# A rotary embedding in fp32: one signed GpSimd product per tile, and PSUM copies of two banks

## The chip, the cores and the metric

One core of a Trainium2 chip runs the kernel. The metric is the device time of one execution in microseconds (us), the median of several runs. The profile's span, from the first to the last instruction of one execution, is about 2 us shorter than that time. Runs come fast or slow; only fast runs are compared.

## The reference

```python
# x: 8 x 2048 x 8 x 64, cos and sin: 2048 x 32, all fp32
x1 = x[..., :32]
x2 = x[..., 32:]
out1 = x1 * cos - x2 * sin
out2 = x1 * sin + x2 * cos
return np.concatenate([out1, out2], axis=-1)
```

Input and output are 33.5 MB each, the tables 0.5 MB together. Every element costs two products and one sum.

## The kernel before

Each of the eight batches is one buffer of 128 x 8192 elements (4.2 MB). SyncE's queue loads five buffers ahead, ScalarE's queue stores each batch from the same buffer, and the load of batch b+5 waits for the store of batch b. A batch is worked off in tiles, most of 2048 elements per partition. PSUM is the memory into which TensorE writes its sums; a bank is here a stretch of it of 512 elements per partition. Of each tile VectorE computes t1 = x * cos and GpSimd t2, the other half of x times sine, with a minus sign for the first half of each head. Then the two are added, in one of three ways:

- kind A: VectorE adds t1 (in PSUM) and t2.
- kind B: TensorE adds them by two matmuls with the identity, and ScalarE copies the sum from PSUM.
- kind C: VectorE computes t2 too; TensorE adds, ScalarE copies. GpSimd has no part.

The first tile of batches 1 and 3 is of kind C, that of batches 2, 4 and 5 of kind B, all others of kind A.

```python
    o_pool = ctx.enter_context(tc.tile_pool(name="op", bufs=2, space=PSUM))
    ...
    keep(nc.scalar.mul(nsin, sin_sb, -1.0))
    keep(nc.scalar.copy(sin_ps, sin_sb))
    ...
        if kind != "C":
            for u, tab in ((1, sin_sb), (0, nsin)):
                keep(
                    nc.gpsimd.tensor_mul(
                        out=t2u[:, :, u, :].rearrange("p (r h) d -> p r h d", h=H),
                        in0=xu[:, :, 1 - u, :].rearrange("p (r h) d -> p r h d", h=H),
                        in1=rep(tab[:, r0 : r0 + nr, :], H),
                    )
                )
        keep(nc.vector.tensor_mul(out=..., in0=xk, in1=rep(cos_ps[...], 2 * H)))   # t1
        if kind == "A":
            keep(nc.vector.tensor_add(out=xt, in0=t1, in1=t2))
        elif kind == "B":
            for j in range(n // C):                       # C = 512 elements, one bank
                o = o_pool.tile([P, C], f32, tag="o")
                cs = slice(j * C, (j + 1) * C)
                nc.tensor.matmul(o, eye, t1[:, cs], start=True, stop=False)
                nc.tensor.matmul(o, eye, t2[:, cs], start=False, stop=True)
                keep(nc.scalar.copy(xt[:, cs], o))
        ...
```

## Time and profile before

| | before |
|---|---|
| time, median of the 3 runs known at first | 164.34 us (164.15 to 164.58) |
| span of the profiled run | 162.0 us |
| busy: VectorE, GpSimd, TensorE, ScalarE | 140.1, 138.9, 46.6, 14.3 us |
| bytes moved | 67.65 MB, mean 418 GB/s |
| 16 DMA engines, both data queues | 98.0% of the span |

Three things are close together here: VectorE, GpSimd and the DMA are all busy for over 85% of the span. A share of the whole span doesn't say which of them sets the end. That takes the view by windows, which shows whether a resource is full in every stretch, and the view of waits, which shows who stands still for whom. The prediction below quotes both.

### The profile page before, as it was taken

How to read it: one execution, taken by the hardware profiler on the slowest of the kernel's cores; microseconds unless marked ns; L12 is line 12 of the kernel's file. 1: busy time of each engine (PE TensorE's matmuls, PEld its weight loads, DVE VectorE, ACT ScalarE, POOL GpSimd, SP SyncE). 2: the span in 40 equal slices, each digit the busy share in tenths (PEclk: the TensorE clock that was granted, in tenths of full speed). 3: DMA queues.
4: the chain of work that ended last, by engine and by line, in shares of the span. 5: the costliest groups of instructions: out<-in, count | busy, mean ns of one | idle time of the engine just before them, and what ended most of it. 6: DMA issues, size and time to landing. Idle time of an engine off the chain costs nothing.

```text
span 162.0 us, 463 instructions
## 1 busy us (share of the span) xinstructions
PE 46.6 (29%) x80; PEld 18.6 (11%) x80; DVE 140.1 (86%) x66; ACT 14.3 (9%) x24; POOL 138.9 (86%) x70
## 2 busy tenths in 40 slices
PE   0000000499008920894039913980000000000000
PEld 0000000143004400340023401330000000000000
DVE  0468999999999999999999999499989999899930
ACT  3200000013100410022001210130000000000000
POOL 1299999999999899983999979999799979999600
PEclk9999999999965997599855895799555555555555
DMA  5999999989899999999999999999999999999994
GB/s 176 419 441 494 413 388 502 372 380 429 388 477 429 396 485 413 405 494 396 421 477 396 429 463 396 453 453 388 453 447 405 445 445 405 453 437 405 417 421 198
DMA packets 3170, 67.65 MB, mean 418 GB/s; under 512 B 352, under 2 KB 352, under 8 KB 608
## 3 DMA queue, kind: packets, MB, share of 16 engines
q1 hardware_dynamic: 1728, 34.08, 49.9%
q10 hardware_dynamic: 1440, 33.56, 48.1%
q14 instruction: 2, 0.02, 0.0%
HBM read 34.08 MB, written 33.55 MB: 417 GB/s over the span
## 4 chain that ended last, share of the span: by engine, by line
DMA 47%; DVE 37%; POOL 9%; issue 2%; SPq 1%; DVEq 0%; POOLq 0%; ACTq 0%
DMA xt<-in_x_dram 26%; DVE t L128 18%; DMA out_dram<-xt 18%; DVE xt L135 17%; POOL t L121 9%; DMA sin_sb<-in_sin_dram 3%; DVE t L145 1%; SPq L69 0%; SPq L67 0%; DVEq L135 0%; POOLq L121 0%; ACTq L74 0%
## 5 line engine op out<-in xcount | busy, mean ns | idle before, releaser
L121 POOL TENSOR_TENSOR t<-xt,sin_sb 128x1024 f32<-128x1024 f32 (+1 forms) x32 | 70.5, 2203 | 12.8 <-DMA xt<-in_x_dram 6.4
L128 DVE TENSOR_TENSOR t<-xt,cos_ps 128x2048 f32<-128x2048 f32 (+1 forms) x34 | 73.4, 2167 | 0.8
L121 POOL TENSOR_TENSOR t<-xt,nsin 128x1024 f32<-128x1024 f32 (+1 forms) x32 | 70.6, 2207 | 0.0
L135 DVE TENSOR_TENSOR xt<-t,t 128x2048 f32<-128x2048 f32 (+1 forms) x29 | 62.2, 2145 | 8.1 <-POOL t L121 5.6
L140 PE MATMUL o<-t,eye 128*128 128x512 f32 x24 | 16.3, 766 | 24.0 <-DVE t L128 24.0
L156 PE MATMUL o<-t,eye 128*128 128x512 f32 x16 | 11.3, 812 | 38.1 <-DVE t L128 38.1
L141 PE MATMUL o<-t,eye 128*128 128x512 f32 x24 | 15.3, 725 | 0.0
L142 ACT COPY xt<-o 128x512 f32<-128x512 f32 x12 | 7.0, 585 | 44.8 <-PE o L141 44.8
L140 PEld LDWEIGHTS o<-t,eye 128*128 128x128 f32 x24 | 5.6, 249 | 32.5 <-issue 32.5
L156 PEld LDWEIGHTS o<-t,eye 128*128 128x128 f32 x16 | 3.8, 257 | 43.0 <-POOL t L121 30.6
L161 ACT COPY xt<-o 128x512 f32<-128x512 f32 x8 | 4.7, 586 | 44.7 <-DVE t L128 26.6
L141 PEld LDWEIGHTS o<-t,eye 128*128 128x128 f32 x24 | 5.7, 239 | 8.0 <-issue 8.0
L92 DVE COPY cos_ps<-cos_sb 128x512 f32<-128x512 f32 x1 | 0.7, 694 | 6.3 <-DMA cos_sb<-in_cos_dram 6.3
L157 PE MATMUL o<-t,neye 128*128 128x512 f32 x8 | 5.3, 766 | 0.2 <-DVE t L145 0.2
L145 DVE TENSOR_TENSOR t<-xt,sin_ps 128x2048 f32<-128x2048 f32 x2 | 4.6, 2281 | 0.0
L157 PE MATMUL o<-t,eye 128*128 128x512 f32 x8 | 4.1, 592 | 0.0
L157 PEld LDWEIGHTS o<-t,neye 128*128 128x128 f32 x8 | 1.9, 258 | 4.1 <-issue 4.1
L157 PEld LDWEIGHTS o<-t,eye 128*128 128x128 f32 x8 | 1.5, 190 | 1.9 <-issue 1.9
L89 ACT ACT_TABLE_LOAD x1 | 1.3, 1283 | 0.7 <-PEq L197 0.7
L89 ACT ACTIVATE nsin<-sin_sb 128x512 f32<-128x512 f32 x1 | 0.6, 629 | 4.9 <-DMA sin_sb<-in_sin_dram 4.9
L90 ACT COPY sin_ps<-sin_sb 128x512 f32<-128x512 f32 x1 | 0.6, 579 | 0.0
L79 POOL MEMSET eye<- 128x128 f32 x1 | 0.2, 204 | 0.3 <-POOLq L197 0.3
(6 smaller groups left out, 1.0 us busy)
## 6 DMA issues: line engine op xcount, KB each, us to landing
xt<-in_x_dram SPq DMA_DIRECT2D x7, 4096.0 KB, 42.0
out_dram<-xt ACTq DMA_DIRECT2D x7, 4096.0 KB, 25.7
xt<-in_x_dram SPq DMA_DIRECT2D x2, 1024.0 KB, 6.1
xt<-in_x_dram SPq DMA_DIRECT2D x1, 2048.0 KB, 11.5
out_dram<-xt ACTq DMA_DIRECT2D x1, 2048.0 KB, 10.8
out_dram<-xt ACTq DMA_DIRECT2D x2, 1024.0 KB, 7.1
cos_sb<-in_cos_dram SPq DMA_DIRECT2D x1, 256.0 KB, 5.1
sin_sb<-in_sin_dram SPq DMA_DIRECT2D x1, 256.0 KB, 5.3
```

Of the source, the lines that this page charges most:

```text
L89: keep(nc.scalar.mul(nsin, sin_sb, -1.0))
L92: keep(nc.vector.tensor_copy(cos_ps, cos_sb))
L121: nc.gpsimd.tensor_mul(out=t2u[:, :, u, :].rearrange("p (r h) d -> p r h d", h=H), in0=xu[:, :, 1 - u, :].rearrange("p (r h) d -> p r h d" ...
L128: nc.vector.tensor_mul(out=t1.rearrange("p (r k d) -> p r k d", r=nr, d=Dh), in0=xk, in1=rep(cos_ps[:, r0 : r0 + nr, :], 2 * H),)
L135: keep(nc.vector.tensor_add(out=xt, in0=t1, in1=t2))
L140: nc.tensor.matmul(o, eye, t1[:, cs], start=True, stop=False)
L141: nc.tensor.matmul(o, eye, t2[:, cs], start=False, stop=True)
L142: keep(nc.scalar.copy(xt[:, cs], o))
L145: nc.vector.tensor_mul(out=t2.rearrange("p (r k d) -> p r k d", r=nr, d=Dh), in0=xk, in1=rep(sin_ps[:, r0 : r0 + nr, :], 2 * H),)
L156: nc.tensor.matmul(o, eye, t1u[:, gs, u, :], start=True, stop=False)
L157: nc.tensor.matmul(o, eye if u else neye, t2u[:, gs, 1 - u, :], start=False, stop=True)
L161: nc.scalar.copy(xu[:, gs, u, :], o.rearrange("p (g d) -> p g d", d=Dh))
```

## The change

The intent is to have GpSimd issue one instruction per tile in place of two, by means of a table that holds minus sine and plus sine in turns and a read of the input that takes the second half of each head first (a step of -32). Besides, ScalarE copies two PSUM banks in one instruction in place of one. For the room this takes, the two PSUM buffers of one bank become one buffer of two banks.

```diff
-    o_pool = ctx.enter_context(tc.tile_pool(name="op", bufs=2, space=PSUM))
+    o_pool = ctx.enter_context(tc.tile_pool(name="op", bufs=1, space=PSUM))
 ... (cos_sb and sin_sb move into a pool that is free at the start)
-    nsin = const_pool.tile([P, R, Dh], f32, tag="ns")
+    sgn = const_pool.tile([P, R, 2, Dh], f32, tag="sg")
 ...
-    keep(nc.scalar.mul(nsin, sin_sb, -1.0))
+    for lo, hi in ((0, 4), (4, R)):
+        keep(nc.scalar.mul(sgn[:, lo:hi, 0, :], sin_sb[:, lo:hi, :], -1.0))
+        keep(nc.scalar.copy(sgn[:, lo:hi, 1, :], sin_sb[:, lo:hi, :]))
 ...
+    def swapped(a, nr):
+        return dataclasses.replace(
+            a,
+            offset=a.offset + Dh,
+            ap=[a.ap[0][:], [HD, nr], [D, H], [-Dh, 2], [1, Dh]],
+        )
+
+    def signed(a, nr):
+        return dataclasses.replace(
+            a, ap=[a.ap[0][:], [D, nr], [0, H], [Dh, 2], [1, Dh]]
+        )
 ...
-            for u, tab in ((1, sin_sb), (0, nsin)):
-                keep(
-                    nc.gpsimd.tensor_mul(
-                        out=t2u[:, :, u, :].rearrange("p (r h) d -> p r h d", h=H),
-                        in0=xu[:, :, 1 - u, :].rearrange("p (r h) d -> p r h d", h=H),
-                        in1=rep(tab[:, r0 : r0 + nr, :], H),
-                    )
+            keep(
+                nc.gpsimd.tensor_mul(
+                    out=t2.rearrange("p (r h u d) -> p r h u d", r=nr, h=H, u=2),
+                    in0=swapped(xt, nr),
+                    in1=signed(sgn[:, r0 : r0 + nr, :, :], nr),
                 )
+            )
 ... (kind B; kind C alike)
-            for j in range(n // C):
-                o = o_pool.tile([P, C], f32, tag="o")
-                cs = slice(j * C, (j + 1) * C)
-                nc.tensor.matmul(o, eye, t1[:, cs], start=True, stop=False)
-                nc.tensor.matmul(o, eye, t2[:, cs], start=False, stop=True)
-                keep(nc.scalar.copy(xt[:, cs], o))
+            for j in range(n // (2 * C)):
+                o = o_pool.tile([P, 2 * C], f32, tag="o")
+                for k in range(2):
+                    cs = slice((2 * j + k) * C, (2 * j + k + 1) * C)
+                    oc = o[:, k * C : (k + 1) * C]
+                    nc.tensor.matmul(oc, eye, t1[:, cs], start=True, stop=False)
+                    nc.tensor.matmul(oc, eye, t2[:, cs], start=False, stop=True)
+                keep(nc.scalar.copy(xt[:, 2 * j * C : 2 * (j + 1) * C], o))
```

More of the change, by code (lines that the diff above doesn't have):

```diff
@@ L46 @@
     t2_pool = ctx.enter_context(tc.tile_pool(name="t2p", bufs=3))
-    cos_sb = const_pool.tile([P, R, Dh], f32, tag="cb")
-    sin_sb = const_pool.tile([P, R, Dh], f32, tag="sb")
-    nsin = const_pool.tile([P, R, Dh], f32, tag="ns")
+    cos_sb = t1s_pool.tile([P, R, Dh], f32, tag="t1s", name="cos_sb")
+    sin_sb = t1s_pool.tile([P, R, Dh], f32, tag="t1s", name="sin_sb")
+    sgn = const_pool.tile([P, R, 2, Dh], f32, tag="sg")
     eye = const_pool.tile([P, P], f32, tag="eye")
@@ L152, in rotate @@
             for u in range(2):
+                o = o_pool.tile([P, n // 2], f32, tag="o")
                 for j in range(n // 2 // C):
-                    o = o_pool.tile([P, C], f32, tag="o")
+                    oc = o[:, j * C : (j + 1) * C]
                     gs = slice(j * G, (j + 1) * G)
-                    nc.tensor.matmul(o, eye, t1u[:, gs, u, :], start=True, stop=False)
+                    nc.tensor.matmul(oc, eye, t1u[:, gs, u, :], start=True, stop=False)
                     nc.tensor.matmul(
-                        o, eye if u else neye, t2u[:, gs, 1 - u, :], start=False, stop=True
+                        oc, eye if u else neye, t2u[:, gs, 1 - u, :], start=False, stop=True
                     )
-                    keep(
-                        nc.scalar.copy(
-                            xu[:, gs, u, :], o.rearrange("p (g d) -> p g d", d=Dh)
-                        )
+                keep(
+                    nc.scalar.copy(
+                        xu[:, :, u, :], o.rearrange("p (g d) -> p g d", d=Dh)
                     )
+                )
     def pieces(b):
```

## The prediction

> **What bounds the kernel now.** GpSimd is the second-busiest engine of the page (138.9 us of a 162.0 us span), and the change works on it, so the first question is whether GpSimd sets the end at all. I read the page's slices and DMA queues first.
>
> ```profile
> POOL 1299999999999899983999979999799979999600
> DMA  5999999989899999999999999999999999999994
> DMA packets 3170, 67.65 MB, mean 418 GB/s; under 512 B 352, under 2 KB 352, under 8 KB 608
> q1 hardware_dynamic: 1728, 34.08, 49.9%
> q10 hardware_dynamic: 1440, 33.56, 48.1%
> ```
>
> To see: the 16 DMA engines are at nine tenths or more in all but four of 40 slices. The two data queues together take 98.0% of the engines' time, 0.98 x 162.0 = 158.8 us. GpSimd has holes (8 and 3 together, then 7, 7, 7), about one every 19 us from the middle on. Is the DMA really full, or full on the average only? The view by windows answers (columns: window, its length, busy time of PE, PEld, DVE, ACT and POOL, granted clock, DMA share, GB/s):
>
> ```profile
> 0.00:5.00 5.00, 0.00 (x0) 0.00 (x0) 0.00 (x0) 1.28 (x1) 0.70 (x6) 1.00 0.64 216
> 5.00:155.00 150.00, 46.65 (x80) 18.60 (x80) 139.83 (x66) 13.06 (x23) 138.24 (x64) 0.76 1.00 430
> 155.00:160.00 5.00, 0.00 (x0) 0.00 (x0) 0.28 (x1) 0.00 (x0) 0.00 (x0) 0.50 0.96 406
> 160.00:162.00 2.00, 0.00 (x0) 0.00 (x0) 0.00 (x0) 0.00 (x0) 0.00 (x0) 0.50 0.03 12
> ```
>
> To see: share 1.00 at 430 GB/s for 150 us on end, and 0.96 until 160. What is not full is the first load's start (5 us at 0.64, so some 1.8 us lost) and the last store's completion (2 us). The 67.65 MB are the input once, the output once and the tables; at 430 GB/s that is 157.3 us, plus these ends of some 4 us: the span. Then the chain that ended last (start, length, what):
>
> ```profile
> 7.03 9.48 POOL t L121 x6
> 16.51 0.02 issue
> 16.53 2.30 DVE xt L135
> ...
> 63.05 28.39 DMA out_dram<-xt
> ...
> 91.57 42.01 DMA xt<-in_x_dram
> ...
> 133.71 4.62 POOL t L121 x2
> ...
> 154.05 1.23 DVE xt L135
> ```
>
> To see: GpSimd stands in it at two places only, 9.5 us at the start and 4.6 us after the last load; in between it is VectorE and then 70 us of one store and one load. The chain names compute after 133.7 us, but the windows show the DMA full there too: it works off stores that wait. The view of GpSimd's waits:
>
> ```profile
> POOL t L121 <- DMA xt<-in_x_dram: 6.4, 4, 3.4
> POOL t L121 <- DMA sin_sb<-in_sin_dram: 5.7, 1, 5.7
> POOL t L121 <- DVE xt L135: 0.5, 1, 0.5
> ```
>
> To see: GpSimd has caught up with the loads in the second half and waits for input, four times, at 75.6, 95.0, 114.4 and 133.7 us by the timeline, 19.36 us apart. Making it faster there only makes it wait longer. **The DMA engines are the bound.**
>
> **What the Trainium skill says.** (1) "DMA: Bandwidth & Descriptors", Specifications, gives a fabric ceiling of 435 GB/s and about 358 GB/s of HBM per core. The trace's 430 GB/s agrees with the first and passes the second, so I take the DMA to be at its ceiling. (2) "GPSIMD Engine Reference", Elementwise — side-by-side cycle accounting, has a two-input fp32 operation over 2048 elements at 4497 ns on GpSimd and 2293 ns on VectorE. The trace has 2292 ns on VectorE; GpSimd runs two instructions of 1024 per tile so far. (3) The same page, Performance pitfalls for Q7 kernels, has reads half again as dear where the inner step is over 8 bytes. The new read's negative step is in the second dimension (-32 elements); the inner step remains one fp32, 4 bytes, so this should not bite. No row of the trace before has a negative step, so it is not tested. (4) "SBUF — State Buffer", Who interferes with whom: a VectorE instruction with two SBUF inputs holds up GpSimd's reads. Here one VectorE input is always in PSUM, and its 2292 ns shows no hindrance; the change leaves that as it is.
>
> **The change part by part.**
>
> *GpSimd.* The groups by form:
>
> ```profile
> L121 POOL TENSOR_TENSOR t<-xt,nsin 128x1024 f32<-128x1024 f32 x28 | 65.6, 2341 | 0.0
> L121 POOL TENSOR_TENSOR t<-xt,sin_sb 128x1024 f32<-128x1024 f32 x28 | 65.4, 2337 | 7.0 <-DMA xt<-in_x_dram 6.4 <-DVE xt L135 0.5
> L121 POOL TENSOR_TENSOR t<-xt,nsin 128x512 f32<-128x512 f32 x4 | 5.1, 1266 | 0.0
> L121 POOL TENSOR_TENSOR t<-xt,sin_sb 128x512 f32<-128x512 f32 x4 | 5.1, 1264 | 5.7 <-DMA sin_sb<-in_sin_dram 5.7
> ```
>
> Records overlap a little, so I count from start to start in the timeline: 2.28 us for 1024 elements, 1.21 us for 512. So 1.07 us per 512 elements and 0.14 us fixed. One instruction of 2048 then starts the next after 0.14 + 4 x 1.07 = 4.42 us, in place of 2 x 2.28 = 4.56: 0.14 us less per tile, since only the fixed part goes; the elements are as many as before. The 64 products become 32 (28 of 2048, 4 of 1024), so 32 x 0.14 = 4.5 us less busy: 138.9 to about 134.4 us. Nearly all of it turns into waits for loads.
>
> *The start.* The first product now needs the signed table. Before, it started when the sine table had landed (7.03 us). Now ScalarE first writes two pieces of 128 elements; the 128-element multiply took 0.30 us, and a second behind it perhaps 0.25. So it starts near 7.5 us, 0.45 late. Then 2.28 + 2.28 + 4.42 = 8.98 us until the third tile's product, at 16.5 us: just where it was (16.51). From there VectorE sets the pace (4.73 us per tile), so the first store is issued at 28.3 us as now. The rest of the table, the PSUM copy of sine and the negated identity are needed only after that.
>
> *TensorE and ScalarE.* A 512-element PSUM copy takes 0.585 us; the 512- and 128-element multiplies (0.629 and 0.299 us) give 0.86 ns per element, so 1024 take about 1.03 us. 20 x 0.585 = 11.7 us become 10 x 1.03 = 10.3. But there is now one PSUM buffer of two banks in place of two of one, so the second pair of chunks waits for the first copy: about 1.1 us of TensorE idle, and a last copy some 1.6 to 2 us later in each of the five tiles. The tightest is batch 4: its last copy ended at 94.6 us; now about 96.2; its store was issued at 97.74, after VectorE's last add. It still fits. The order of instructions and their waits on GpSimd and TensorE are otherwise those of before, tile for tile; the same one waits for TensorE to release a product buffer.
>
> *The end.* After 155.0 us the windows have 406 x 5 + 12 x 2 = about 2.05 MB still moving. The last store, 1.05 MB, is issued at 155.28, so some 0.9 MB of earlier stores, 2.1 us, lie before it. Less its own start, perhaps 1 us, the last add has about 1 us in hand. It comes 0.14 us earlier through the first product after the last load: hidden in that backlog. Sum: nothing off the path that sets the end, nothing on it; -0.1 to +0.2 us.
>
> **The rivals.** (A) *GpSimd is a co-bound and its saving counts.* For: 86% busy, in the chain at both ends. Were it the bound, 4.5 us would go, to about 160. Against: the DMA share of 1.00 and the waits for loads. Without fewer bytes this cannot be; I give it 1%. (B) *The four-dimensional read with its negative step is slow on GpSimd.* A tile may take 19.36 / 4 = 4.84 us before GpSimd falls behind the loads, 9% over my 4.42. At half as much again, 6.6 us, 30 tiles' worth alone are 198 us and the kernel ends near 210; at 5.2 us, 7.5 + 30 x 5.2 = 164 us of product plus some 10 us of tail, about 172. Nothing in the profile speaks for it, and nothing tests it: 4%. (C) *The single PSUM buffer delays a store.* TensorE's first matmuls of a tile run at half speed (0.85 us against 0.43 in the timeline), and if the new gap makes the second half slow too, 3.4 us more pass: batch 4's store would be issued near 99.6, 2 us late. Until 133.6 us loads keep the DMA busy beside the stores, so this should cost 0 to 0.5 us.
>
> **Range and chances.** I expect 164.3 us, the median of before. Three runs spread over 0.43 us; with (C) and a little of the ends, 163.7 to 165.1. Faster by over 2% needs less than 161.1 us, which would be a span with no start and no end: 0.01. Slower is (B) in its bad forms: 0.04. Within 2%: 0.95.
>
> **What would show it right or wrong.** Right: 32 GpSimd products, the large ones near 4.45 us, GpSimd busy near 134.5 us and its waits for loads up by some 4 us; first product near 7.5 us; first store issued near 28.3; PSUM copies near 1.03 us; DMA share still 1.00 at 430 GB/s between 5 and 155 us. Wrong: large products over 4.84 us (B); a drop of the DMA share in the middle, behind a late copy (C); a DMA rate well off 430 GB/s at a full share, which none of this foresees.

## The result

The changed kernel took 164.01 us (median of 6 runs, 163.83 to 164.46), the kernel before 164.25 us on the same chip (6 runs). The ratio is 0.9987, with a 95% interval of 0.997 to 1.0005: the same. Ratios here and below are the mean time of one kernel's fast runs over that of the other's of the same rounds, so they are not quite the ratio of the medians that are quoted.

The groups by form of the changed kernel (busy time, mean ns of one, idle time before them and who ended it):

```profile
L134 POOL TENSOR_TENSOR t<-xt,sgn 128x2048 f32<-128x2048 f32 x28 | 125.8, 4525 | 9.6 <-DMA xt<-in_x_dram 7.9 <-DVE xt L148 1.6
L134 POOL TENSOR_TENSOR t<-xt,sgn 128x1024 f32<-128x1024 f32 x4 | 9.3, 2346 | 6.3 <-ACT sgn L91 6.3
L157 ACT COPY xt<-o 128x1024 f32<-128x1024 f32 x6 | 6.1, 1012 | 45.9 <-PE o L156 32.5 <-DVE t L141 13.5
```

The change did what it was meant to do: there are 32 products for 64, and copies of 1024 elements. GpSimd's busy time went from 138.9 to 135.7 us. The three waits at the ends of the two POOL rows show where the 3.2 us went. GpSimd's waits for loads rose from 6.4 to 7.9 us, those for buffers from 0.5 to 1.6, and the first product waits for the signed table, until 7.62 us in place of 7.03. Together that is 3.2 us more of waiting.

The view by windows of the changed kernel (window, length, busy time of PE, PEld, DVE, ACT, POOL, granted clock of TensorE as a share of full speed, DMA share, that is the mean busy share of the 16 DMA engines, GB/s):

```profile
0.00:5.00 5.00, 0.00 (x0) 0.00 (x0) 0.00 (x0) 1.28 (x1) 0.70 (x6) 1.00 0.62 220
5.00:155.00 150.00, 47.56 (x80) 17.88 (x80) 139.49 (x66) 12.18 (x16) 135.02 (x32) 0.77 1.00 429
155.00:160.00 5.00, 0.00 (x0) 0.00 (x0) 0.62 (x1) 0.00 (x0) 0.00 (x0) 0.50 0.98 415
160.00:162.50 2.50, 0.00 (x0) 0.00 (x0) 0.00 (x0) 0.00 (x0) 0.00 (x0) 0.50 0.05 20
```

The DMA is as full as before: a share of 1.00 at 429 GB/s for 150 us. In the chain that ended last (start, length, what) the pieces are the same too, each a little later:

```profile
7.62 1.92 POOL t L134
...
63.30 28.47 DMA out_dram<-xt
...
91.89 42.12 DMA xt<-in_x_dram
...
134.14 4.52 POOL t L134
...
154.39 1.23 DVE xt L148
```

The last add begins at 154.39 us, 0.34 us later than before. The two profiled executions themselves took 164.40 and 164.16 us, although the medians of the kernels agree, so this pair alone doesn't say what a shift of the chain costs. In e1_product_only (below) the last add begins at 153.63 us, 0.42 us earlier than before, at the same span of 162.0 us. The experiments ask how large a shift moves nothing.

### The profile page after: what moved, and what is told of

Same layout as the page of the kernel before. It is cut to its first block, busy times and chain, and to the rows that moved or that the text cites. A ratio compares the mean times of both kernels' runs of the same rounds, so it can differ in the third digit from the quotient of the medians.

```text
span 162.5 us, 428 instructions
## 1 busy us (share of the span) xinstructions
PE 47.6 (29%) x80; PEld 17.9 (11%) x80; DVE 140.1 (86%) x66; ACT 13.5 (8%) x17; POOL 135.7 (84%) x38
## 4 chain that ended last, share of the span: by engine, by line
DMA 47%; DVE 36%; POOL 8%; issue 4%; SPq 1%; ACT 0%; DVEq 0%; POOLq 0%; ACTq 0%
DMA xt<-in_x_dram 26%; DVE t L141 18%; DMA out_dram<-xt 18%; DVE xt L148 16%; POOL t L134 8%; DMA sin_sb<-in_sin_dram 3%; DVE t L160 1%; SPq L69 0%; SPq L67 0%; ACT sgn L90 0%; DVEq L148 0%; ACT sgn L91 0%; POOLq L134 0%; ACTq L74 0%
## 5 line engine op out<-in xcount | busy, mean ns | idle before, releaser
L134 POOL TENSOR_TENSOR t<-xt,sgn 128x2048 f32<-128x2048 f32 (+1 forms) x32 | 135.0, 4253 | 15.9 <-DMA xt<-in_x_dram 7.9
L155 PE MATMUL o<-t,eye 128*128 128x512 f32 x24 | 16.5, 778 | 23.7 <-DVE t L141 20.3
L172 PE MATMUL o<-t,eye 128*128 128x512 f32 x16 | 10.8, 760 | 39.2 <-DVE t L141 37.0
L156 PE MATMUL o<-t,eye 128*128 128x512 f32 x24 | 14.9, 708 | 0.0
L157 ACT COPY xt<-o 128x1024 f32<-128x1024 f32 x6 | 6.1, 1012 | 45.9 <-PE o L156 32.5
L177 ACT COPY xt<-o 128x1024 f32<-128x1024 f32 x4 | 4.0, 1012 | 46.6 <-PE o L173 46.6
L173 PE MATMUL o<-t,neye 128*128 128x512 f32 x8 | 6.2, 863 | 0.2
L173 PE MATMUL o<-t,eye 128*128 128x512 f32 x8 | 4.1, 592 | 0.0
L90 ACT ACTIVATE sgn<-sin_sb 128x128 f32<-128x128 f32 (+1 forms) x2 | 0.8, 414 | 5.0 <-DMA sin_sb<-in_sin_dram 5.0
L91 ACT COPY sgn<-sin_sb 128x128 f32<-128x128 f32 (+1 forms) x2 | 0.8, 388 | 0.0
```

The source lines that it names most:

```text
L90: keep(nc.scalar.mul(sgn[:, lo:hi, 0, :], sin_sb[:, lo:hi, :], -1.0))
L91: keep(nc.scalar.copy(sgn[:, lo:hi, 1, :], sin_sb[:, lo:hi, :]))
L134: nc.gpsimd.tensor_mul(out=t2.rearrange("p (r h u d) -> p r h u d", r=nr, h=H, u=2), in0=swapped(xt, nr), in1=signed(sgn[:, r0 : r0 + nr, ...
L155: nc.tensor.matmul(oc, eye, t1[:, cs], start=True, stop=False)
L156: nc.tensor.matmul(oc, eye, t2[:, cs], start=False, stop=True)
L157: keep(nc.scalar.copy(xt[:, 2 * j * C : 2 * (j + 1) * C], o))
```

## The experiments

The theory to be tested: **the transfers are the bound**, GpSimd's saving turns into waits, and what the change adds is hidden. The rivals: GpSimd is a co-bound, so its time counts; the late PSUM copy takes back a gain; the swapped read costs something that hides a gain. Where nothing else is said, an edit is made to the changed kernel, and the result is right. The kernel before was run beside each set (medians 164.30 us for e1 to e4, 164.26 for e5 to e8, 164.18 for e9 to e12), and the ratios are against it. The changed kernel was not timed again, so a difference against its 164.01 us carries about 0.1 us more of doubt.

### Each half of the change alone

e1_product_only takes the GpSimd half, with the PSUM buffers and copies of before; e2_psum_only takes the PSUM half, with the two products of before. The edits are the two halves of the diff above; e1_product_only against the changed kernel:

```diff
-    o_pool = ctx.enter_context(tc.tile_pool(name="op", bufs=1, space=PSUM))
+    o_pool = ctx.enter_context(tc.tile_pool(name="op", bufs=2, space=PSUM))
 ... (kinds B and C: matmuls and copies as in the kernel before)
```

and e2_psum_only against the kernel before:

```diff
-    o_pool = ctx.enter_context(tc.tile_pool(name="op", bufs=2, space=PSUM))
+    o_pool = ctx.enter_context(tc.tile_pool(name="op", bufs=1, space=PSUM))
 ... (kinds B and C: matmuls and copies as in the changed kernel)
```

> Half of the change alone: one GpSimd product per tile over the signed table, PSUM copies as before. Transfers theory: the time stays within 0.4 us of the kernel before (163.8 to 164.6), GpSimd busy about 135.7 us. Rival (GpSimd a co-bound): about 3 us, its saved busy time, come off, near 161. Last copy of each TensorE tile as early as before.

> The other half alone: one PSUM buffer of two banks and half as many ScalarE copies, two GpSimd products per tile as before. Transfers theory: 163.8 to 164.6 us although the last copy of each TensorE tile comes 1.5 to 2 us later. Rival (a late copy holds back a store): 0.5 to 2 us slower.

e1_product_only took 164.52 us (163.95 to 164.8) against 164.30 for the kernel before: ratio 1.0011 (0.9995 to 1.0028). GpSimd was busy for 135.8 us, as expected, and the time did not follow. The rival's 161 us are excluded.

e2_psum_only took 163.91 us (163.84 to 164.12): ratio 0.9973 (0.9959 to 0.9986). The late copy costs nothing; in the timeline, batch 4's store follows VectorE's last add, not the copy. That this half came out 0.4 us shorter, and clear of noise by its interval, was not expected. GpSimd and VectorE have nearly the same busy times in it as before (139.0 and 140.1 us), and its DMA share is the same. I have no cause for it; see e12 below. The ratios of the two halves multiply to 0.9984, close to the 0.9987 of the whole change.

### Half of GpSimd's work

The product is computed for half of each tile and used twice (wrong result, 0.68 relative error).

```diff
-            t2 = t2_pool.tile([P, n], f32, tag="t2")
+            t2 = t2_pool.tile([P, n // 2], f32, tag="t2")
-        t2u = t2.rearrange("p (g u d) -> p g u d", u=2, d=Dh)
+        if kind == "C":
+            t2u = t2.rearrange("p (g u d) -> p g u d", u=2, d=Dh)
-                    out=t2.rearrange("p (r h u d) -> p r h u d", r=nr, h=H, u=2),
-                    in0=swapped(xt, nr),
-                    in1=signed(sgn[:, r0 : r0 + nr, :, :], nr),
+                    out=t2.rearrange("p (r h u d) -> p r h u d", r=nr // 2, h=H, u=2),
+                    in0=swapped(xt[:, : n // 2], nr // 2),
+                    in1=signed(sgn[:, r0 : r0 + nr // 2, :, :], nr // 2),
-            keep(nc.vector.tensor_add(out=xt, in0=t1, in1=t2))
+            twice = dataclasses.replace(t2, ap=[t2.ap[0][:], [0, 2], [1, n // 2]])
+            keep(
+                nc.vector.tensor_add(
+                    out=xt.rearrange("p (w m) -> p w m", w=2),
+                    in0=t1.rearrange("p (w m) -> p w m", w=2),
+                    in1=twice,
+                )
+            )
-                    nc.tensor.matmul(oc, eye, t2[:, cs], start=False, stop=True)
+                    hs = slice(k * C, (k + 1) * C)
+                    nc.tensor.matmul(oc, eye, t2[:, hs], start=False, stop=True)
```

> Wrong result on purpose: GpSimd computes only half of each tile's product, which is used twice; GpSimd busy falls from 135.7 to about 70 us. Transfers theory: time unmoved, 163.6 to 164.5 us, DMA share still 1.00 between 5 and 155 us. Rival (GpSimd a co-bound): at least 5 us faster, down to where VectorE's 140 us of work plus start and tail set the end.

It took 164.05 us (163.7 to 164.44): ratio 0.9981 (0.9964 to 0.9998). The page of this run has the busy times (us, share of the span, instructions):

```profile
PE 48.2 (30%) x80; PEld 18.2 (11%) x80; DVE 140.2 (86%) x66; ACT 13.5 (8%) x17; POOL 71.1 (44%) x38
```

and the view of GpSimd's waits:

```profile
POOL t L135 <- DMA xt<-in_x_dram: 55.1, 8, 10.6
POOL t L135 <- DVE xt L151: 13.3, 7, 4.4
```

GpSimd's work fell by 64.6 us (71.1 in place of 135.7), and 58.9 us of that reappear as waits for loads and buffers (68.4 in place of 9.5). This settles the first rival: even halving GpSimd's work is worth nothing that can be told from noise in this kernel.

### The transfers alone, and fewer bytes

e4_transfers_only drops all computing and keeps every load and store in its pieces and on its queue (wrong result):

```diff
-    nc.gpsimd.memset(eye, 0.0)
 ... (the identity, the tables in SBUF and PSUM and all of rotate are deleted too)
-            rotate(b, lo, n)
```

e8_less_stored computes everything, but leaves out 2.1 MB of stores (incomplete result):

```diff
-        outs = list(spans([2 * UNIT, UNIT, UNIT] if b == last else [ROW]))
+        outs = list(spans([2 * UNIT, UNIT, UNIT] if b == last else [2 * UNIT] if b == 3 else [ROW]))
```

> Wrong result on purpose: the same loads, table loads and stores in the same pieces, no computing. Transfers theory: this is the floor, 163.0 to 164.5 us, at 429 to 430 GB/s. Rival (computing sets part of the time): several us under 164, at most 160.

> Incomplete result on purpose: the second half of batch 3, 2.1 MB of 67.6, is computed but not stored. Transfers theory: 2.1 MB at 430 GB/s, so 4.9 us faster, near 159.2 us. Rival (computing sets the end): time unmoved, since all computing is still done.

The transfers alone took 163.22 us (162.96 to 164.01), ratio 0.9937, and the DMA was as full as with the computing (here the columns are POOL's busy time, the clock, the share and GB/s):

```profile
5.00:155.00 150.00, 0.00 (x0) 1.00 1.00 430
```

So the whole of the computing adds about 1 us to what moving the bytes takes. As far as these runs show, this is the floor for a change that leaves the bytes, the pieces and the rate of the transfers as they are, and the kernel before was already within about 1 us of it.

With 2.1 MB fewer, the time was 160.12 us, ratio 0.9748, 4.1 us less than before. The theory said 4.9. The windows of this run tell where 0.8 us stayed:

```profile
5.00:150.00 145.00, 47.83 (x80) 18.01 (x80) 136.84 (x64) 12.17 (x16) 134.93 (x32) 0.78 1.01 430
150.00:155.00 5.00, 0.00 (x0) 0.00 (x0) 3.27 (x3) 0.00 (x0) 0.00 (x0) 0.50 0.69 292
```

After 150 us the DMA is no longer full: it waits for VectorE, whose last add ends at 153.4 us, with the last store still to come. So the second bound seems to be VectorE, only some 4 us behind the first: from 103.2 us to the last add this run's chain holds nothing but its products and adds, with less than 0.2 us between them. No edit of VectorE's work tests this.

### More work on GpSimd

An unused product follows each product, of 64 elements in e5_more_64 and of 256 in e6_more_256 (the same edit with 256):

```diff
+    junk = const_pool.tile([P, 64], f32, tag="junk")
+            jk = sgn[:, 0:4, :, :].rearrange("p r u d -> p (r u d)")[:, :64]
+            keep(nc.gpsimd.tensor_mul(out=junk, in0=jk, in1=jk))
```

> The changed kernel with one more GpSimd product of 64 elements (unused) behind each of the 32 products: about 0.22 to 0.27 us each, 7 to 8.6 us of GpSimd work added, twice what the change took away. The trace of the changed kernel has 9.5 us of GpSimd waits for loads and buffers after its first product. Transfers theory: these waits shrink to 1 to 3 us and the time stays under 164.8 us. Rival (GpSimd a co-bound): about 7 us slower.

> The same with 256 elements: about 0.62 to 0.68 us each, 20 to 22 us of GpSimd work added, more than the 9.5 us of waits. Here both theories have GpSimd set the end: the slack theory says 10 to 13 us slower (174 to 177 us), a co-bound without slack would be 20 us slower (184 us).

With 64 elements: 164.06 us (5 runs from 163.9 to 164.09, one of 165.89), ratio 1.0004 (0.9972 to 1.0037). GpSimd was busy for 143.6 us, 7.9 more than in the changed kernel and 4.7 more than before, and its waits for loads and buffers had shrunk from 9.5 to 2.5 us:

```profile
POOL t L135 <- DMA xt<-in_x_dram: 1.8, 2, 1.4
POOL t L135 <- DVE t L144: 0.7, 1, 0.7
```

From start to start a full tile took 4.72 us.

With 256 elements: 168.21 us (168.08 to 168.35), ratio 1.0237. Here GpSimd waits for nothing any more after its first product, and the timeline shows 5.04 us from one tile to the next (start, length, engine, line, operation):

```profile
139.63 4.52 POOL L135 TENSOR_TENSOR t<-xt,sgn 128x2048 f32<-128x2048 f32 x1
144.09 0.63 POOL L142 TENSOR_TENSOR junk<-sgn 128x256 f32<-128x256 f32 x1
144.66 4.52 POOL L135 TENSOR_TENSOR t<-xt,sgn 128x2048 f32<-128x2048 f32 x1
...
154.74 2.37 POOL L135 TENSOR_TENSOR t<-xt,sgn 128x1024 f32<-128x1024 f32 x1
157.05 0.63 POOL L142 TENSOR_TENSOR junk<-sgn 128x256 f32<-128x256 f32 x1
```

Both theories of this expectation were too high. The account: 31 added products of 0.57 us lie ahead of the last one, 17.7 us. Of these 9.5 us replace waits, which leaves about 8. The last product starts 7.7 us later by the timeline, the last add 6.1 us later, since the product had been ready some 2 us before VectorE needed it. The time grew by 4.2 us over the changed kernel. The last 2 us were hidden by stores that were still waiting when the last add ended. The expectation had counted the waits only, not these two margins. This brackets the threshold and agrees with the prediction: 4.72 us per tile cost nothing, 5.04 us cost 4.2 us, and the 4.84 us at which GpSimd was to fall behind the loads lie between.

### Is the swapped read dear?

```diff
-                    in0=swapped(xt, nr),
+                    in0=xt.rearrange("p (r h u d) -> p r h u d", r=nr, h=H, u=2),
```

> Wrong result on purpose: the product reads the input in plain order (no swap, no negative step). If the swapped read with its negative step costs nothing, the 128x2048 product keeps its 4525 ns; if it is what makes the product dearer than the 4.42 us start to start that was predicted, it falls by about 0.06 us or more. Time unmoved either way.

One look, 164.05 us (one run, so its state is unknown; wrong result on purpose). The group by form, as above:

```profile
L134 POOL TENSOR_TENSOR t<-xt,sgn 128x2048 f32<-128x2048 f32 x28 | 125.7, 4517 | 9.8 <-DMA xt<-in_x_dram 8.2 <-DVE xt L148 1.7
```

4517 ns against 4525: reading in plain order saves 8 ns of a product, 0.2%. The negative step in the second dimension is all but free.

### How much lateness the start and the end can hide

e11_last_twice issues the first product after the last load twice, so that nothing can be caught up. e12_first_later computes half of the very first product once more ahead of it. e10_first_twice issues the whole of the first product twice. e9_tables_on_act was a try at the 5 us of the start in which the DMA isn't full: it issues the table loads from the other queue.

e11_last_twice:

```diff
-            keep(
+            for _ in range(2 if (b, lo) == (last, 0) else 1):
+              keep(
```

e12_first_later, ahead of the product:

```diff
+        if (b, lo) == (0, 0):
+            keep(
+                nc.gpsimd.tensor_mul(
+                    out=t2[:, :HD].rearrange("p (r h u d) -> p r h u d", r=1, h=H, u=2),
+                    in0=swapped(xt[:, :HD], 1),
+                    in1=signed(sgn[:, 0:1, :, :], 1),
+                )
+            )
```

e10_first_twice:

```diff
-            keep(
+            for _ in range(2 if (b, lo) == (0, 0) else 1):
+              keep(
```

e9_tables_on_act:

```diff
-                keep(nc.sync.dma_start(out=cos_sb, in_=cos_src))
-                keep(nc.sync.dma_start(out=sin_sb, in_=sin_src))
+                keep(nc.scalar.dma_start(out=cos_sb, in_=cos_src))
+                keep(nc.scalar.dma_start(out=sin_sb, in_=sin_src))
```

> The changed kernel with the first product after the last load issued twice: 4.5 us more, where the chain shows GpSimd for 4.5 us and nothing can be caught up later. VectorE's last add moves from 155.6 to about 160.1. If the chain's reading is the price: 4.5 us slower. Prediction's 1 us in hand: 3.5 us slower (167.5). If the whole 2 us of earlier stores still to be moved count, as the run with 256 more elements suggests: about 2.5 us slower (166.5).

> The changed kernel with half of the very first GpSimd product (512 elements, about 1.2 us) computed once more ahead of it, so that all of batch 0 and its store come 1.2 us later. The run with the tables on ScalarE's queue had its first product 3.2 us later and took 1.5 us longer at a full share of the transfers. If lateness at the start is paid in part (about half), 164.6 us; if it is free as the strict transfers theory has it, 163.8 to 164.4; if the chain's reading is the price, 165.2. If many runs fall in a slow state as with the first product issued twice, only the fast ones count.

> The changed kernel with the very first GpSimd product issued twice: 2.3 us more at the start, where the chain that ended last shows GpSimd for some 9 us. If that piece of the chain sets the end: about 2.3 us slower (166.3). Transfers theory: the first store is issued 2 us later (near 30.5), the loads fill the transfers meanwhile, and the time stays within 0.4 us of the changed kernel.

> The changed kernel with the two table loads issued from ScalarE's queue, so that SyncE issues the input loads one right behind the other. If the 5 us at the start, in which the transfers have a share of 0.62, are bound by the order of issuing (two issues of 0.42 us ahead of the second input load), 0.2 to 0.6 us come off (163.4 to 163.8). If it is the first transfer's own delay, the time stays at 164.0.

**The end.** e11_last_twice took 167.14 us (166.9 to 167.32), ratio 1.0176, 3.1 us more than the changed kernel's 164.01. Its timeline has the last add at

```profile
159.34 1.23 DVE L149 TENSOR_TENSOR xt<-t,t 128x1024 f32<-128x1024 f32 x1
```

which is 4.95 us later than in the changed kernel (154.39). So 4.95 - 3.1 = 1.9 us were hidden (2.0 by the spans of the two profiled executions, 165.4 and 162.5 us), about the 2 us of the whole backlog of stores and twice the 1 us of the prediction. The expected 2.5 us differ only because the add came 4.95 and not 4.5 us later. Together with the run of 256 elements (6.1 - 4.2 = 1.9 us) this measures the margin at the end twice.

**The start.** e12_first_later has its first full product at 8.90 in place of 7.62 us, and its first store is issued at 29.82 in place of 28.55 us. It took 163.68 us (163.52 to 164.11), ratio 0.9969 (0.9956 to 0.9983). 1.3 us of lateness at the start are free, as the theory has it. That it took even 0.5 us less than the kernel before is a difference of the same kind as e2_psum_only's: at an unchanged DMA share, and without a cause that I could name.

**Two runs that the strict theory does not explain.** e10_first_twice, 2.3 us later at the start, gave one fast run of 165.29 us and five slow ones (169.85 to 172.18). There is no ratio for one fast run, and slow runs are not explained here, so it shows nothing for sure. No other version had a slow run, so the edit may bring them on; that is open too, and lateness at the start is shown to be free for 1.3 us only. e9_tables_on_act took 165.56 us (165.03 to 166.19), ratio 1.0081. Its sine table came late, 9.0 us after it was issued in place of 5.4, probably because more of the input was issued alongside it: the first product began at 10.79 us. But that cannot be all, for the DMA was full from 5 us on. The windows of the changed kernel first, then of this run:

```profile
50.00:100.00 50.00, 28.21 (x48) 10.37 (x46) 48.45 (x22) 6.07 (x6) 43.20 (x11) 0.80 1.00 433
```

```profile
50.00:100.00 50.00, 30.35 (x48) 11.47 (x48) 48.43 (x23) 6.07 (x6) 45.10 (x11) 0.79 1.00 426
```

At the same share of 1.00 the DMA moved 426 GB/s here and 433 there. Over 50 us that is 0.35 MB, or 0.8 us. Before 50 us it goes the other way, so that 430 and 428 GB/s remain for 5 to 150 us, about 0.3 MB or 0.7 us of the 1.6 us between the two spans (162.5 and 164.1 us). The view counts a packet's bytes where the packet starts. When they are spread over the packet's own time, every other fast profile has 432 to 433 GB/s between 50 and 100 us, and this one 426: the difference isn't blur. By the same count the rate is 409 to 420 GB/s at a full share between 28 and 50 us, after the first stores, in every profile with computing. So a full share is not quite a fixed rate. What moves it is not shown: that it is the order in which loads and stores meet is a guess that no run isolates. This stays open, and with it the 0.3% by which e2_psum_only and e12_first_later came out shorter. No version with a right result beat the kernel before by more than this.

## Why the prediction was right

The time lay 0.3 us from the 164.3 predicted, within the range. By the steps of the prediction:

- **The DMA engines are the bound.** Right, and shown: half of GpSimd's work less left the time as it was (e3), the transfers alone need 163.2 us (e4), and 2.1 MB fewer saved 4.1 us (e8).
- **GpSimd's saving.** The mechanism was right: a fixed part per instruction goes, and it turns into waits. Its size was off. From start to start the large product takes (17.97 - 4.53) / 3 = 4.48 us, from four in a row in the timeline, not 4.42. About 0.08 us per tile are saved, not 0.14, and the busy time fell by 3.2 us, not 4.5. The fixed part of 0.14 us held: in the new form 1024 elements take 2.31 us from start to start (154.74 to 157.05 in e6's timeline above), and 2 x 2.31 - 4.48 = 0.14. The added products of 64 and 256 elements, 0.25 and 0.57 us from start to start, give 0.14 too (0.25 - 64 x 0.32 / 192). The term that failed is the cost per element, which the prediction took over from the old form: 1024 elements took 2.28 us there, so 512 more cost 1.07 us in the old form and (4.48 - 2.31) / 2 = 1.09 us in the new. The swapped read is not the cause (e7); which other part of the new form is, stays open.
- **The start.** The first product began at 7.62 us (predicted: near 7.5), the first store was issued at 28.55 us (28.3). The 0.25 us of lateness were still there at the fourth store (81.74 in place of 81.50 us) and cost nothing; e12 shows that five times as much is free.
- **TensorE and ScalarE.** The copy took 1.01 us (1.03); batch 4's last copy ended at 96.6 us (96.2). Its store was issued at 98.40, after VectorE's last add that ended at 98.31. The copy wasn't waited for, as predicted.
- **The end.** The direction was wrong in a detail: the last add came 0.34 us later, not 0.14 earlier, as the loads before it had landed later. The term "about 1 us in hand" was mis-sized: two runs measure about 2 us.
- **The rivals.** (A) falls with e3. (B) falls with e7; its estimate for a slower product holds, for with e6's 5.04 us it gives 7.5 + 30 x 5.04 + 10 = 169 us against 168.2 measured. (C) falls with e2.

## What to carry to other kernels

An engine that is busy for 86% of the span, and even stands in the chain that ended last, can be worth nothing to speed up: look first whether another resource is full in every window, and whether the engine already waits for that resource. A run of the transfers alone costs little and gives the floor at once; here it was 1 us under the kernel, so only fewer bytes or a better rate of the transfers could have brought much more than that. How much lateness a kernel hides is found by adding work, at one place and in two doses, rather than by taking some away.

## What the Trainium skill lacked or had wrong

- "DMA: Bandwidth & Descriptors", Specifications: the table gives about 358 GB/s of HBM per core without a condition, and Where 436 GB/s comes from says that this side binds for transfers between HBM and SBUF. It does not here: with loads and stores mixed on one core, the runs show 429 to 430 GB/s over 150 us, near the fabric ceiling of the same table. The page's own note under its measured figures has it right, that the 358 GB/s are the share when both cores of a pair stream. Nor does the page say how far the rate of fully busy DMA engines varies: between 50 and 100 us the runs show 426 and 433 GB/s at the same share of 1.00, in kernels of 165.56 and 164.01 us.
- "GPSIMD Engine Reference", Performance pitfalls for Q7 kernels and Elementwise — side-by-side cycle accounting: the page gives no cost for a negative step in an outer dimension, and no figure for the whole fixed cost of one instruction, only "tens of cycles" for one step of its dispatch. The runs show 4525 ns with the negative step and 4517 ns in plain order, and from start to start 4.48 us for one instruction of 2048 elements against 2 x 2.31 us for two of 1024 in the same form, so 0.14 us per instruction.
